# The low part of a weight piece made by one subtraction of 1024 columns, in place of two of 512

## The chip, the cores and the metric

The kernel runs on one core of a Trainium2 chip, as one program. The metric is the time of one execution on the device, in microseconds (us); the span is the part of it that the profiler covers. The engines are TensorE (PE; PEld is its weight load), VectorE (DVE), ScalarE (ACT), GpSimd (POOL) and SyncE (SP), which here only issues transfers. Each engine works through its own instructions in order and waits for others by semaphores.

## What is computed

Two layers of a decoder trunk on 256 tokens with 1024 features, all in float32:

```python
mod = silu(c) @ w_ada + b_ada;  shift, scale, gate = split(mod, 3)
h = rms_norm(x, pre_g) * (1 + scale) + shift
qa, ka, va, ga, qb, kb, vb, gb = split(h @ w_in)      # 8 chunks of 512 columns
# partial rotary on q and k; 8 heads of 64 in each branch
o_a = mixture_of_three_causal_windows(qa, ka, va) * silu(ga)
o_b = causal_block_attention(qb, kb, vb) * silu(gb)   # 256 tokens: one block
y = rms_norm(concat(o_a, o_b) @ w_out, post_g)
x = x + gate * y
```

## The kernel before, in words

**Weights.** All weights lie in HBM as float32 and are read once, 70 MB in all. SP loads them in pieces of 512 KB, `raw` of 128 partitions x 2 k-tiles x 512 columns, into a ring of 6 buffers (line 121 for W_in and W_out, line 142 for W_ada). A piece is only loaded once the piece six before it has been read for the last time, mostly by DVE.

**The split.** TensorE multiplies float32 weights here as two parts. `split_piece` (line 198) has ACT make the high part `whi`, a copy in a shorter format of all 1024 columns (line 205), and calls `split_low` (line 209), which has DVE make the low part, `wlo = raw - whi` (line 212). There are 9 buffers for `whi`, 8 for `wlo`. Each k-tile then takes three matmuls of 512 columns: whi with the high part of h, whi with its low part, wlo with the high part (`product`, line 513; for the gate chunks with weights and h changed over, line 526; in the start line 753). In the start some pieces are split one half at a time, by steps `f` and `g` of a list; later `split_half` takes whole pieces.

**Modulation.** Pieces of W_ada are not multiplied on TensorE. DVE folds each, scaled by silu(c), into an accumulator (line 364, `acc_g` for the gate and `acc_ss` for shift and scale, 1024 columns each), and then ACT and DVE split the gate's sum and TensorE adds it up (lines 444 to 455).

**A head pair.** The stages of a pair of heads hang together over four engines. T: PE transposes q and k into one bank of PSUM (line 571), of which there are two; ACT copies (`qkh` 577, `qkT` 578), DVE makes `qkl` (579), which frees the bank. S: PE makes scores (592, 595). DVE adds the mask and takes the row's minimum (`z`, `den`, 601); ACT takes Exp with sums (604); DVE takes the reciprocal (`rc`, 608) and scales three of four blocks of z (614), ACT the fourth (612). X: PE transposes z in two groups of three (625) into the same two banks, so the second group waits for the `qkl` of the next pair; ACT copies (`pT`, 628). V: PE makes outputs (642), ACT copies them (650). When the gate chunk is there, ACT makes `gs` with Silu (561), DVE multiplies (660), ACT and DVE split (667, 668). Exp and Silu stand in different tables of ACT, so a change between them costs a table load, which the profile shows as ACT_TABLE_LOAD with the line of the instruction behind it.

**Order.** The start, about 60 us, is written out for all engines. After it, only PE's order is that of the program text: products in slots, with stages T, S, X and V of eight head pairs a layer at set slots. The orders of DVE, ACT, POOL and SP are made by the framework's scheduler from its own estimates of when operands are ready, so that a change in one instruction can change the order of others. Layer 0's eight head pairs lie at about 63 to 153 us, the layer boundary at 153 to 190, layer 1 at 190 to 315.

Of the kernel before, what the change touches and what calls it, by code (L numbers as in the profile page):

```python
# [9 lines left out]
F32 = mybir.dt.float32  # L10
# [8 lines left out]
RD = 16  # L19
RH = RD // 2  # L20
EPS = 1e-6
BIG = 1e30
# Slots: one product of half a chunk each, counted in a layer up to 32. Pairs of values: one for each layer.
# Where the heads of a branch start, and the distance of scores, transposes and outputs from there
AT_A, AT_B = ((12, 10), (22, 22))
# where branch A is gated; where the gate and the second token tile's h are made
AO = (28, 27)
AO2 = (0, 2)
GATE_D = (3, 1)
OS, OX, OV = ((1, 1), (3, 3), (4, 5))  # L30
# buffers for weights as loaded and for their two parts
NRAW, NHI, NLO = (6, 9, 8)
FOLD = 2048
# how far the splitting of weights runs ahead; what goes to the scalar engine; where W_ada's parts are due
AHEAD = (-12, 4)
# [3 lines left out]
ADA0, ADA1, ADA2 = ((2, 1), (6, 1), (23, 2))  # L39
# The start. GROUPS: k-tiles whose modulation is made together. FIRST_LOADS: a, b W_ada of a group, f a k-tile of  # L40
# W_in for the first two chunks, s, v quarters of chunks 2 and 5. FIRST_STEPS: T small inputs, R rotary tables, K masks,
# n, x norm and transposes of x, a, b, m modulation of a group, h, l its h in two parts, f, g a weight piece in two
# parts, p its products, w, y and s, v the same for chunks 2 and 5, k products that keep the array busy.
GROUPS = ((0, 1), (1, 1), (2, 2), (4, 2), (6, 2))
# [5 lines left out]
GATE_AT = (21, 27)  # L50
# theta ** (-2 i / RD) in float32
INV_FREQ = [1.0, 0.1939227432012558, 0.03760603070259094, 0.007292664609849453,
# [4 lines left out]
def turn_constants():  # L57
    """For units 2^20, 2^8, 2^-4: frac(unit / 2 pi) cut into parts of 12 bits, over the unit."""
    from fractions import Fraction
    pi = Fraction("3.14159265358979323846264338327950288419716939937510582097494459230781640628620899")  # L60
    rows = []
    for e in (20, 8, -4):
        u = Fraction(2) ** e
        f = u / (2 * pi)
        f -= f.numerator // f.denominator
        f1 = Fraction((f * 4096).numerator // (f * 4096).denominator, 4096)
        g = f - f1
        f2 = Fraction((g * 2 ** 24).numerator // (g * 2 ** 24).denominator, 2 ** 24)
        f3 = g - f2
        rows.append([float(f1 / u), float(f2 / u), float(f3 / u)])  # L70
    return rows
# [3 lines left out]
def trunk(ctx: ExitStack, tc: tile.TileContext, x, c, positions, pre_gain, post_gain,  # L75
# [18 lines left out]

    # ---------------------------------------------------------------- small inputs
    # rows: positions, c, the gains of the first norm, the shift and scale parts of b_ada
    NR = NT + KT + L * KT + 2 * L * KT
# [13 lines left out]

    # ---------------------------------------------------------------- weight stream
    raw_q = {}
# [5 lines left out]
    def load_weights(src, key, r0, c0):  # L119
        """Two k-tiles of 512 columns"""  # L120
        nc.sync.dma_start(piece(key), src[r0:r0 + 2 * P, c0:c0 + CW].rearrange("(k p) n -> p k n", p=P))

    def load_first(key):
        """A k-tile for the first two chunks"""
        k = key[1]
        nc.sync.dma_start(piece(key).rearrange("p c n -> p (c n)"), w_in[0, k * P:(k + 1) * P, 0:2 * CW])

    def load_group(key):
        """W_ada's columns for the shift and scale of a group of features: some of the rows"""
        _, g, q = key  # L130
# [7 lines left out]
    def load_ada(key):  # L138
        """i < KT: a k-tile, the shift or the scale of all features; else the gate, a k-tile"""
        _, l, i, s = key  # L140
# [23 lines left out]

    # Order of the weight stream: with each layer's products, what the next modulation needs.
    # a, b: W_ada for a group of features; f: the rows of W_in that it scales; s, v: quarters of other chunks
    stream = []
    for x in FIRST_LOADS.split():
# [6 lines left out]
        else:  # L175
            stream.append(("in", 0, 2 if i == "s" else 5, g, m))
    # what the modulation needs, after the halves named
    ADA_AT = {}
# [19 lines left out]
    def split_piece(key, a, b, low=True):  # L198
        """Parts a to b of a piece: hi holds the first 12 bits of each weight, lo the other 12."""
        load_upto(key)  # L200
# [8 lines left out]
    def split_low(key, a, b):  # L209
        raw, hi, lo = raw_q[key], hi_q[key], lo_q[key]  # L210
        for d in range(a, b):
            nc.vector.tensor_sub(lo[:, d, :], raw[:, d, :], hi[:, d, :].bitcast(F32))  # L212

# [4 lines left out]

    # ---------------------------------------------------------------- constants
    ident = cp.tile([P, P], F32, name="ident")  # L220
# [5 lines left out]
    dummy = cp.tile([P, 1], F32, name="dummy")  # L226
    # the table set of Silu serves until the first Exp
    nc.scalar.activation(dummy, nhalf, AF.Silu)
    onesr = cp.tile([P, P], F32R, name="onesr")
    nc.scalar.activation(onesr, ones, AF.Copy)  # L230

    # masks, to be added to minus the scores: [queries 0-127 x keys 0-127 | queries 128-255 x keys 0-255]
    NS = P + S
# [29 lines left out]

    # silu(c) and the gains of the first norm by feature on partitions
    cs = cp.tile([P, KT], F32, name="cs")
# [18 lines left out]
    def make_rope():  # L284
        # rotary tables: the angle in turns, reduced exactly, for any position
        invf = cp.tile([P, RH], F32, name="invf")
# [46 lines left out]

    # ---------------------------------------------------------------- modulation
    acc, mod = {}, {}
# [30 lines left out]
    def mod_of(l, part, nb=4):  # L366
        """Rows 0, 32, .. of part in columns: [feature in its block, block, row]."""
        pm = ps.tile([P, CW], F32, name="t", bufs=2)
# [10 lines left out]
    def ada_sum(l):  # L379
        """Sums over partitions of acc; 512 features to each group of 32 columns of the array."""  # L380
        assert all((l, i) in folded for i in range(KT))
# [66 lines left out]
    def gate_end(l, h):  # L448
        """Sums over partitions of acc, on every partition, times the gain of the second norm."""
        pm = ps.tile([P, CW], F32, name="o", bufs=1)  # L450
# [5 lines left out]

    # ---------------------------------------------------------------- norms
    def rstd_of(ms, other=None):
        """(sum of means + EPS) ** -0.5"""
        e = ap.tile([P, 2], F32, name="rstd", bufs=4)  # L460
# [9 lines left out]
    def parts_of(l, g):  # L470
        """hi and lo of half the features of h (or of a branch's output), for all tokens"""
        if (l, g) not in hT:
# [30 lines left out]

    # ---------------------------------------------------------------- products with weights
    def product(bank, act, t, key, first, last, part=None):
        """The four k-tiles of a half, or two of them."""
        if key + (0 if part is None else part,) not in hi_q:
# [8 lines left out]
    def gate_product(bank, act, u, key, hf):  # L516
        """Features 256 u to 256 (u + 1) of a chunk on partitions, all tokens: the weights stay, h streams."""
        if key + (0,) not in hi_q:
# [10 lines left out]

    # ---------------------------------------------------------------- attention  # L530
    qk, vv, gs, qkT, oo = {}, {}, {}, {}, {}
# [35 lines left out]
    def st_T(br, p):  # L567
        pt = ps.tile([P, CW], F32, name="t", bufs=2)
        for i in range(2):
            for t in range(NT):  # L570
                nc.tensor.transpose(pt[:, (2 * i + t) * P:(2 * i + t + 1) * P],
                                    qk[br, i][:, t, p * P:(p + 1) * P], ident)
        # the first 128 queries and keys; for the others, queries and all keys in two parts
        d = ap.tile([P, 2, P], F32, name="qkT", bufs=2)
# [59 lines left out]
    def st_V(br, p):  # L634
        """Outputs of two heads: [feature, token]"""
        res = pT.pop((br, p))
# [18 lines left out]
    def finish(br, p, src=None):  # L655
        """Outputs of two heads times the gate, in two parts"""
        heads.remove((br, p))
# [36 lines left out]

    # ---------------------------------------------------------------- the program
    xT, xn0 = [], []
# [45 lines left out]
    def first_product(q, j, ci):  # L742
        """k-tile 2 q + j with chunk ci, both token tiles"""
        whi, wlo = hi_q["first", 2 * q + j], lo_q["first", 2 * q + j]
# [13 lines left out]
    def early(t, part):  # L758
        """The first half of chunk 5, kept in the memory until the second one is due."""
        if not parked:  # L760
# [32 lines left out]
    def keep_clock(n):  # L793
        """Products that nothing reads: the array's clock stays down until it has been busy for a while."""
        pt = ps.tile([P, CW], F32, name="s", bufs=2)
# [133 lines left out]
```

## Time and profile before

| | us |
|---|---|
| median of 3 runs | 322.24 (322.04 to 323.86) |
| span of the profiled execution | 321.5 |
| PE busy | 299.6 (93%) |
| DVE busy | 245.6 (76%) |
| ACT busy | 203.5 (63%) |
| DVE, the 160 subtractions of line 212 | 102.4 |
| ACT, the 88 copies of line 205 | 84.4 |

A row of a timeline gives start, duration, engine, line, operation, out<-in with sizes; in brackets the idle time before it and who ended it. [...] The granted clock of TensorE was at its higher level (1.00) in all stretches that matter here.

### The profile page before, as it was taken

Reading aid. Unit: us, or ns where it says so; the run is one execution under the profiler, and the core shown is the slowest. Engines: PE = TensorE matmul, PEld = TensorE weight load, DVE = VectorE, ACT = ScalarE, POOL = GpSimd, SP = SyncE. Lnnn points to the kernel's source line nnn. Section 1 sums busy time; section 2 is a strip of 40 time slices with the busy share of each in tenths; the row PEclk is TensorE's granted clock in tenths of the full one; section 3 lists DMA queues with packets and bytes.
Section 4 is the critical chain, followed back from the end, with each engine's and each line's share of the span. In section 5 each row is a group of like instructions: output and inputs, shape, how many; then the busy total and the mean of one; then the engine's idle time right before and its main releaser. Section 6 shows DMA issues by size and latency. Waiting matters only on the chain.

```text
span 321.5 us, 5293 instructions
## 1 busy us (share of the span) xinstructions
PE 299.6 (93%) x1817; PEld 237.6 (74%) x1817; DVE 245.6 (76%) x637; ACT 203.5 (63%) x435; POOL 12.3 (4%) x46
## 2 busy tenths in 40 slices
PE   0898899989999999999999899999999999999992
PEld 0565475867777789877687688877777799997881
DVE  4866773998998989898879899789785566786122
ACT  3646161959777469879568457578675579984100
POOL 3100001000000000000020300000000000000001
PEclk9999999999999999999999999999999999999998
DMA  8999988899798787586858549997765433000011
GB/s 253 342 351 302 346 262 308 293 348 317 247 302 265 259 287 202 173 280 233 285 185 282 178 129 303 350 320 231 228 215 177 132 132 131 2 1 2 0 65 65
DMA packets 37394, 70.63 MB, mean 220 GB/s; under 512 B 2492, under 2 KB 12790, under 8 KB 37368
## 3 DMA queue, kind: packets, MB, share of 16 engines
q1 hardware_dynamic: 36960, 69.22, 65.7%
q10 hardware_dynamic: 408, 1.09, 0.9%
q8 instruction: 14, 0.23, 0.3%
q14 instruction: 12, 0.10, 0.1%
HBM read 69.24 MB, written 1.05 MB: 219 GB/s over the span
## 4 chain that ended last, share of the span: by engine, by line
PE 57%; DMA 14%; DVE 13%; ACT 10%; issue 2%; SPq 1%; POOL 1%; ACTq 0%; DVEq 0%; POOLq 0%
PE mm L513 31%; PE mm L526 7%; DMA raw<-in_w_in_dram 5%; DVE wlo L212 4%; DMA raw<-in_w_ada_dram 4%; ACT whi L205 4%; DMA raw<-in_w_out_dram 3%; PE mm L753 3%; ACT z L604 3%; PE o L642 3%; PE o L414 2%; PE t L625 2%; DVE acc_ss L364 2%; DMA rows<-in_b_ada_dram 1%; PE t L513 1%
## 5 line engine op out<-in xcount | busy, mean ns | idle before, releaser
L212 DVE TENSOR_TENSOR wlo<-raw,whi 128x512 fp32r<-128x512 f32 x160 | 102.4, 685 | 8.0 <-PE mm L513 3.1
L205 ACT ACTIVATE whi<-raw 128x1024 fp32r<-128x1024 f32 (+1 forms) x88 | 84.4, 979 | 37.2 <-DMA raw<-in_w_in_dram 19.8
L513 PE MATMUL mm<-whi,hi 128*128 128x512 f32 x200 | 81.7, 408 | 0.0
L513 PE MATMUL mm<-wlo,hi 128*128 128x512 f32 x200 | 79.1, 395 | 0.0
L513 PE MATMUL mm<-whi,lo 128*128 128x512 f32 x200 | 79.0, 395 | 0.0
L513 PEld LDWEIGHTS mm<-whi,hi 128*128 128x128 f32 x200 | 37.6, 188 | 10.5 <-issue 1.7
L513 PEld LDWEIGHTS mm<-wlo,hi 128*128 128x128 f32 x200 | 37.6, 188 | 8.8
L513 PEld LDWEIGHTS mm<-whi,lo 128*128 128x128 f32 x200 | 37.7, 189 | 8.1 <-DVE lo L502 0.5
L526 PE MATMUL mm<-hi,whi 128*128 128x256 f32 x128 | 37.2, 291 | 0.0
L526 PE MATMUL mm<-hi,wlo 128*128 128x256 f32 x128 | 36.1, 282 | 0.0
L526 PE MATMUL mm<-lo,whi 128*128 128x256 f32 x128 | 36.0, 281 | 0.0
L604 ACT ACTIVATE z<-z,den 128x128 f32<-128x128 f32 x64 | 28.3, 445 | 3.8 <-DVE den L601 3.8
L526 PEld LDWEIGHTS mm<-hi,whi 128*128 128x128 f32 x128 | 24.1, 188 | 1.2 <-issue 0.2
L526 PEld LDWEIGHTS mm<-lo,whi 128*128 128x128 f32 x128 | 24.2, 189 | 0.2
L526 PEld LDWEIGHTS mm<-hi,wlo 128*128 128x128 f32 x128 | 24.1, 188 | 0.0
L364 DVE SCALAR_TENSOR_TENSOR acc_g<-raw,cs,acc_g 128x1024 f32<-128x1024 f32 x16 | 20.5, 1281 | 4.1 <-DMA raw<-in_w_ada_dram 4.1
L687 DVE TENSOR_TENSOR tmp<-mm,gate 128x512 f32<-128x512 f32 x8 | 5.5, 688 | 16.8 <-ACT sq L685 16.8
L364 DVE SCALAR_TENSOR_TENSOR acc_ss<-raw,cs,acc_ss 128x1024 f32<-128x1024 f32 x14 | 17.5, 1276 | 0.0
L685 ACT ACTIVATE sq<-mm 128x512 f32<-128x512 f32 x8 | 4.7, 593 | 19.8 <-PE mm L513 19.8
L625 PE MATMUL t<-ident,z 128*128 128x128 f32 x96 | 15.0, 282 | 2.4 <-DVE qkl L579 1.1
L625 PEld LDWEIGHTS t<-ident,z 128*128 128x128 f32 x96 | 10.6, 140 | 6.2 <-issue 1.7
L628 ACT ACTIVATE pT<-t 128x384 f32<-128x384 f32 x32 | 14.0, 491 | 1.2 <-PE t L625 1.2
(173 smaller groups left out, 454.9 us busy)
## 6 DMA issues: line engine op xcount, KB each, us to landing
raw<-in_w_in_dram SPq DMA_DIRECT2D x64, 512.0 KB, 5.2
raw<-in_w_ada_dram SPq DMA_DIRECT2D x32, 512.0 KB, 4.7
raw<-in_w_ada_dram SPq DMA_DIRECT2D x32, 256.0 KB, 5.0
raw<-in_w_out_dram SPq DMA_DIRECT2D x16, 512.0 KB, 5.1
xs<-in_x_dram SPq DMA_DIRECT2D x2, 512.0 KB, 4.3
gate<-in_post_norm_gain_dram ACTq DMA_DIRECT2D x2, 512.0 KB, 4.9
out_dram<-xs SPq DMA_DIRECT2D x4, 256.0 KB, 2.1
rows<-in_b_ada_dram ACTq DMA_DIRECT2D x2, 8.0 KB, 4.9
```

What stands on the lines that cost most here:

```text
L205: nc.scalar.activation(hi_q[key][:, a:b, :], raw[:, a:b, :], AF.Copy)
L212: nc.vector.tensor_sub(lo[:, d, :], raw[:, d, :], hi[:, d, :].bitcast(F32))
L364: nc.vector.scalar_tensor_tensor(a[:, sl], r[:, sl], cs[:, k:k + 1], a[:, sl], op0=ALU.mult, op1=ALU.add)
L414: nc.tensor.matmul(pm[32 * j:32 * j + 32, :w], csz[:, k, :], r[:, i * w:(i + 1) * w], start=k < 4, stop=k >= 4, tile_position=(0, 32 * j))
L513: nc.tensor.matmul(bank, a[:, k, t, :], w[:, k % 2, :], start=first and k + i == 0, stop=last and k == KH - 1 and i == 2)
L526: nc.tensor.matmul(bank[:, b * S:(b + 1) * S], w[:, k % 2, c0:c0 + P], a[:, k].rearrange("p t q -> p (t q)"), start=hf + b + k + i == 0, s ...
L604: nc.scalar.activation(z[:, a:b], z[:, a:b], AF.Exp, bias=den[:, 0, t, i:i + 1], scale=-1.0, accum_out=den[:, 1, t, i:i + 1])
L625: nc.tensor.transpose(pt[:, b * P:(b + 1) * P], pp[i][:, b * P:(b + 1) * P], ident)
L628: nc.scalar.activation(d, pt[:, :NS], AF.Copy)
L642: nc.tensor.matmul(ob[i * HD:(i + 1) * HD, q0:q0 + P], v[:, t, h], res[i][:, c0:c0 + P], start=t == 0, stop=n != 1, tile_position=(0, i * HD))
L687: nc.vector.tensor_mul(yg[:, sl], yb.pop((t, cc)), gate[l][:, sl])
L753: nc.tensor.matmul(mm[0, ci, t], a[:, k, t, :], w[:, ci, :], start=q == 0 and j == 0 and i == 0, stop=q == 3 and j == 1 and i == 2)
```

## The change

In `split_low` the loop over the k-tiles of a piece is gone: one `tensor_sub` takes all the columns that the call is for. For a whole piece that is 1024 columns in place of two times 512. Calls for one half (steps `g` of the start) stay as they are.

```diff
     def split_low(key, a, b):
         raw, hi, lo = raw_q[key], hi_q[key], lo_q[key]
-        for d in range(a, b):
-            nc.vector.tensor_sub(lo[:, d, :], raw[:, d, :], hi[:, d, :].bitcast(F32))
+        nc.vector.tensor_sub(lo[:, a:b, :], raw[:, a:b, :], hi[:, a:b, :].bitcast(F32))
```

Comments were taken out at the same time; from line 212 on, a line's number is one lower than before. The order of PE's and of SP's instructions is the same in both kernels. Those of DVE and ACT differ.

On ACT at the first head pair of layer 0 the order was this (`vv` is the copy of a value chunk; the rows from the table load on are Exp, then the copies of the next pair's q and k):

```order
L557 ACTIVATE vv<-t 128x512
L205 ACTIVATE whi<-raw 128x1024
L604 ACT_TABLE_LOAD
L604 ACTIVATE z,den<-z,den 128x128
L604 ACTIVATE z,den<-z,den 128x256
L604 ACTIVATE z,den<-z,den 128x128
L604 ACTIVATE z,den<-z,den 128x256
L577 ACTIVATE qkh<-t 128x384
L578 ACTIVATE qkT<-t 128x256
L205 ACTIVATE whi<-raw 128x1024
L612 ACTIVATE z<-z,rc 128x256
```

It is now this, with the second `whi` ahead of the table load, where it stood behind the copies of q and k:

```order
L556 ACTIVATE vv<-t 128x512
L205 ACTIVATE whi<-raw 128x1024 x2
L603 ACT_TABLE_LOAD
L603 ACTIVATE z,den<-z,den 128x128
L603 ACTIVATE z,den<-z,den 128x256
L603 ACTIVATE z,den<-z,den 128x128
L603 ACTIVATE z,den<-z,den 128x256
L576 ACTIVATE qkh<-t 128x384
L577 ACTIVATE qkT<-t 128x256
L205 ACTIVATE whi<-raw 128x1024
L611 ACTIVATE z<-z,rc 128x256
```

On DVE at the same pair, from behind its `den` on, the order was this (the numbers tell buffers apart: raw_889 and raw_891 are pieces of W_ada, raw_994 and raw_1001 the two next weight pieces):

```order
L364 SCALAR_TENSOR_TENSOR acc_g_795<-raw_889,cs_108,acc_g_795 128x1024
L212 TENSOR_TENSOR wlo_997<-raw_994,whi_996 128x512
L364 SCALAR_TENSOR_TENSOR acc_g_795<-raw_891,cs_108,acc_g_795 128x1024
L608 RECIPROCAL rc_770<-den_759 128x4
L212 TENSOR_TENSOR wlo_997<-raw_994,whi_996 128x512
L614 TENSOR_SCALAR z_760<-z_760,rc_770 128x128
L614 TENSOR_SCALAR z_760<-z_760,rc_770 128x256
L614 TENSOR_SCALAR z_765<-z_765,rc_770 128x128
L579 TENSOR_TENSOR qkl_819<-t_812,qkh_818 128x384
L212 TENSOR_TENSOR wlo_1004<-raw_1001,whi_1003 128x512 x2
L364 SCALAR_TENSOR_TENSOR acc_g_795<-raw_1008,cs_108,acc_g_795 128x1024
```

It is now this (raw_881, raw_984, raw_990 and raw_996 are the former raw_891, raw_994, raw_1001 and raw_1008). The split of the second piece has moved ahead of `rc`, and a fold stands between `rc` and the three z:

```order
L363 SCALAR_TENSOR_TENSOR acc_g_787<-raw_881,cs_108,acc_g_787 128x1024
L211 TENSOR_TENSOR wlo_987<-raw_984,whi_986 128x1024
L211 TENSOR_TENSOR wlo_993<-raw_990,whi_992 128x1024
L607 RECIPROCAL rc_764<-den_753 128x4
L363 SCALAR_TENSOR_TENSOR acc_g_787<-raw_996,cs_108,acc_g_787 128x1024
L613 TENSOR_SCALAR z_754<-z_754,rc_764 128x128
L613 TENSOR_SCALAR z_754<-z_754,rc_764 128x256
L613 TENSOR_SCALAR z_759<-z_759,rc_764 128x128
L578 TENSOR_TENSOR qkl_811<-t_804,qkh_810 128x384
```

On ACT at the sixth pair, where the first Silu of layer 0 comes behind that pair's Exps, the order was this (raw_1788 is the first piece of W_out):

```order
L604 ACTIVATE z_1399,den_1393<-z_1399,den_1393 128x256
L561 ACT_TABLE_LOAD
L561 ACTIVATE gs_1458<-mm_1286 128x512
L612 ACTIVATE z_1399<-z_1399,rc_1404 128x256
L650 ACTIVATE oo_1467<-o_1460 128x256
L577 ACTIVATE qkh_1475<-t_1469 128x384
L578 ACTIVATE qkT_1474<-t_1469 128x256
L667 ACTIVATE hi_1609<-oo_922 128x256 x2
L205 ACTIVATE whi_1790<-raw_1788 128x1024
```

It is now this (raw_1764 is the former raw_1788). That piece's `whi` stands ahead of the table load; the same has happened at the eighth pair with a later piece:

```order
L603 ACTIVATE z_1381,den_1375<-z_1381,den_1375 128x256
L205 ACTIVATE whi_1766<-raw_1764 128x1024
L560 ACT_TABLE_LOAD
L560 ACTIVATE gs_1438<-mm_1270 128x512
L611 ACTIVATE z_1381<-z_1381,rc_1386 128x256
L649 ACTIVATE oo_1447<-o_1440 128x256
L576 ACTIVATE qkh_1455<-t_1449 128x384
L577 ACTIVATE qkT_1454<-t_1449 128x256
```

## Rows read from the trace of the kernel before

**Rows 1.** Busy time by stretch: from:to, length, each engine (count), PE's clock, DMA share.
```profile
63.00:153.00 90.00, 86.97 (x612) 71.63 (x611) 83.88 (x220) 67.92 (x158) 0.95 (x1) 1.00 0.82 266
...
190.00:315.00 125.00, 124.63 (x782) 103.40 (x780) 85.68 (x229) 81.46 (x175) 0.86 (x2) 1.00 0.45 148
...
sum 321.50, PE 299.62 PEld 237.64 DVE 245.65 ACT 203.47 POOL 12.30; mean PE 59.92 PEld 47.53 DVE 49.13 ACT 40.69 POOL 2.46
```

**Rows 2.** Waits of PE, 63 to 153 us: total, times, longest.
```profile
PE t L571 <- DVE qk L550: 1.0, 1, 1.0
PE t L625 <- DVE z L614: 0.8, 2, 0.5
PE t L625 <- DVE qkl L579: 0.7, 3, 0.3
PE t L625 <- ACT z L612: 0.4, 1, 0.4
```

**Rows 3.** Waits of PE, 190 to 315 us.
```profile
PE t L625 <- DVE qkl L579: 0.4, 1, 0.4
```

**Rows 4.** Waits of DVE, 63 to 153 us.
```profile
DVE rc L608 <- ACT z L604: 3.7, 4, 1.4
```

**Rows 5.** The page's costliest groups: count, busy, mean ns, idle time before.
```profile
L212 DVE TENSOR_TENSOR wlo<-raw,whi 128x512 fp32r<-128x512 f32 x160 | 102.4, 685 | 8.0 <-PE mm L513 3.1
```

**Rows 6.** The chain of waits, 55 to 163 us, rows for prices: start, us, what.
```profile
90.73 1.20 DVE acc_g L364
...
120.45 2.41 DVE wlo L212 x4
...
134.24 0.34 DVE oo L660
```

**Rows 7.** Busy time by stretch, line 212 alone.
```profile
63.00:153.00 90.00, 26.50 (x41) 1.00 0.82 266
```

**Rows 8.** Timeline of DVE at the end of layer 0.
```profile
158.18 3.10 DVE L212 TENSOR_TENSOR wlo<-raw,whi 128x512 fp32r<-128x512 f32 x5
```

**Rows 9.** Timeline of PE at the end of layer 0.
```profile
161.74 0.40 PE L513 MATMUL mm<-wlo,hi 128*128 128x512 f32 x1
```

**Rows 10.** The chain of waits at head 0.
```profile
72.27 1.06 ACT whi L205
...
73.35 1.28 ACT L604
...
76.55 0.18 DVE rc L608
...
77.22 0.73 DVE z L614 x3
77.96 0.48 DVE qkl L579
```

**Rows 11.** Timeline of SP, the issue of the second piece at head 0.
```profile
68.58 0.38 SPq L121 DMA_DIRECT2D raw<-in_w_in_dram  x1
```

**Rows 12.** Transfers of line 121 from 67 to 76 us.
```profile
DMA to landing us min/median/max: 4.5/4.5/5.1
```

**Rows 13.** The chain of waits at heads 4 to 7.
```profile
115.64 0.95 ACT whi L205
116.59 1.37 ACT z L604 x6
...
125.79 5.31 DMA raw<-in_w_out_dram
...
148.15 0.41 ACT z L612
```

**Rows 14.** Timeline of PE at head 0, the second transposes of z.
```profile
78.48 0.33 PE L625 MATMUL t<-ident,z 128*128 128x128 f32 x1 [0.22 <-DVE qkl L579]
```

**Rows 15.** Timeline of ACT at head 5.
```profile
125.74 1.28 ACT L561 ACT_TABLE_LOAD   x1
```

## The prediction, made blind

> **What bounds the kernel now.** I read the busy time by stretches first [rows 1]. Over the whole span TensorE (PE) is busy 299.6 of 321.5 us, VectorE (DVE) 245.65. The stretches say where that mean comes from: in 63 to 153 us (layer 0 after its hand-ordered start, eight head pairs, called heads 0 to 7 here) PE is busy 86.97 of 90 us and DVE 83.88; in 190 to 315 (layer 1) PE is busy 124.63 of 125 and DVE only 85.68. So layer 1 is PE's alone, and layer 0 is shared: PE is nearly full, and DVE has 6 us to spare in 90.
>
> Next I read what PE waited for. In 63 to 153 its waits add up to 2.9 us: 1.0 for the last rotary result (qk, L550), 0.8 and 0.4 for the scaled probabilities z of a head (DVE L614, ACT L612), 0.7 for qkl (L579) [rows 2]. In all of layer 1 it is 0.4 [rows 3]. PE never waits for wlo, the very thing that the change makes. What a faster subtraction can give is therefore only what it lets DVE do sooner for the heads; and DVE's own largest wait in that stretch is for ACT's Exps, 3.7 us [rows 4], which the change does not speed up.
>
> **The price of the new instruction.** Before, 160 subtractions of 128x512 take 102.4 us, 685 ns of duration each [rows 5]. What one costs DVE is the distance to the next start: four in a row take 2.41 us, so 0.60 each; a tensor-by-tensor operation of 256 columns takes 0.34 [rows 6]. Between the two, 256 columns more cost 0.26; so 1024 columns cost 0.60 + 2 x 0.26 = 1.13, against 1.20 for two of 512. That saves 0.08 a pair. The nearest row of that width is a fold (L364, 1024 columns, two operands and a factor): 1.20 [rows 6], which would save nothing. I take 1.13, since the narrower rows are of the same operation; the bounds are 0 and 0.08. Of the 160, 16 are single halves of the start and stay; 72 pairs are merged: 72 x 0.08 = 5.8 us of DVE in all. In 63 to 153, where DVE is nearly full, lie 41 subtractions [rows 7], some 20 pairs: 1.6 us. In layer 1 it is idle time on an engine that already has 39 us of it: 0.
>
> What a merged subtraction loses is an early first half: the low part of the first k-tile is there 1.13 - 0.60 = 0.53 later than before. That matters where wlo is used soon after it is made. The tightest place is the end of layer 0: five subtractions in a row end at 161.28 [rows 8], the last two of them a pair, and PE uses the first of that pair at 161.74 [rows 9]. Merged, both halves are ready when the second one is now, still 0.46 ahead of the use. So I count 0 there; at worst, with a split that comes later in the new order, 0.5.
>
> [...]
>
> **The order.** The larger part of the change is not in its line. PE's and SP's orders are hand-set or stay the same; DVE's and ACT's are made by the framework's scheduler, and they come out otherwise (the excerpts above). Three places count.
>
> Head 0. On ACT a second whi now stands ahead of the table load for Exp. Before, the load began at 73.35, right behind the first whi (72.27) [rows 10]. The second whi's piece was issued at 68.58 [rows 11] and lands 4.5 to 5.1 later [rows 12]: 73.1 to 73.7. A whi holds ACT for 0.95 (115.64 in [rows 13]), so the load begins at 74.2 to 74.6, 0.8 to 1.3 later, and the reciprocal rc moves from 76.55 to about 77.7. On DVE a fold (1.20) now stands between rc and the three z (L614), where before it was the rest of a 512 subtraction: rc to z took 77.22 - 76.55 = 0.67 and now takes 0.09 + 1.20 = 1.29, which is 0.6 more. Behind z stands qkl of head 1, and PE's second group of transposes (78.48) waits for it, because it needs the bank that qkl frees. PE already waited 0.22 there [rows 14], so the whole delay shows: 1.4 to 1.9; I take **+1.7**.
>
> Heads 1 to 6. In heads 1 to 3 the z stand 1 to 2 us of DVE work later in the order, but PE comes 1.7 later too and had no wait at any of the three: 0. At heads 4 to 6 PE's waits of before for z (0.8) and for qkl (0.7 [rows 2], of which 0.2 at head 0) are covered by PE's own lateness: 0.8 + 0.7 - 0.2 = **-1.3**.
>
> Head 5. On ACT a whi of W_out stands ahead of the table load for Silu, which began at 125.74 [rows 15]; its piece was issued only at 125.79, when a fold of DVE had freed its buffer, and took 5.31 to land [rows 13]. In the new order that fold stands ahead of head 5's scores on DVE, where before it stood behind them. Counted from head 4's rc, before it come a split, z, qkl and a gate product: 1.13 + 0.73 + 0.48 + 0.60 + 1.20 for the fold itself = 4.1. That rc follows the Exps, which ended at 117.97 with a whi of 0.95 in their midst [rows 13] that now stands elsewhere: rc at 117.0 to 118.0, fold done at 121.2 to 122.1, piece landed at 126.5 to 127.4, whi done 0.95 later, and the load 1.7 to 2.6 late. I take 1.8. PE is late itself by then (1.7 less 0.3 for head 4 and 0.3 for head 5, of the above); the rest is new: **+0.7**. With a piece that lands at 131.1, as before, it would be +5.
>
> Head 7. A whi again stands ahead of the Silu load, behind which come gs and the z of ACT at 148.15 [rows 13]. PE waited for that z already, the 0.4 in [rows 2], so a whi of 0.95 shows whole: **+0.9**.
>
> The start: four merged splits, each of which waits for its whi and not for DVE; at most 4 x 0.08: **-0.1**. Layer 1: **0**; a split now stands ahead of z at its first head, where the only wait of PE lies [rows 3], so at worst +0.5.
>
> Sum: 1.7 - 1.3 + 0.7 + 0.9 - 0.1 = +1.9. The profiled execution has a span of 321.5; the median of the runs is 322.2, 0.7 above it. 321.5 + 1.9 + 0.7 = **324.1 us**.
>
> **The rivals.**
> A, DVE's time comes back. The orders matter little, and DVE hands the heads over sooner: PE's waits in layer 0 (2.9) go, and the 0.3 of the start: 322.2 - 3.2 = 319.0; half of it gives 320.6. For it: DVE is busy 83.88 of 90 us in that stretch [rows 1], and 1.5 of the waits are on its z and qkl. Against: these stand behind ACT's Exps, and the first 1.0 is for rotary work right behind the start's merged splits, which wait for their whi. Chance 0.10. [...]
> B, nothing moves. PE's stream covers both the gain and the new order; then 321.2 to 322.8. For it: waits of 3 us in 90 say that the slack is small, but at heads 1 to 3 it is there. Against: at head 0 PE had no slack at all. Also the case where the merged operation costs the fold's 1.20 and the scheduler's moves cancel. Chance 0.20.
> C, as worked out: a loss at heads 0, 5 and 7, half returned at 4 to 6: 322.8 to 325.5. Chance 0.45.
> D, slower. The whi at head 5 waits for its piece in front of the Silu load. It decides once the piece lands after about 127; each us later is a us of PE, since the load, gs, z and qkl of the next head follow one another on ACT. At 129 to 131 it gives 322.2 + 1.7 + 2 to 5 = 326 to 329. For it: ACT's largest waits in this stretch are for pieces, and before, this one came at 131.1. Against: its buffer is freed earlier in the new order. Chance 0.25.
>
> **How the numbers follow.** 324.1 is C's. About 1% (3.2 us) is what a measurement of this kernel tells from no change: 319.0 to 325.5. Below 319.0 lies the better half of A, 0.05; above 325.5 lies D, 0.25; the rest, 0.70, is within. The range 320.5 to 327.0 leaves out most of A (0.07) and half of D (0.12). C's own range is 322.8 to 325.5.
>
> **What would show it.** In the new profile: a merged subtraction with a duration of about 1.22 us and a distance of 1.13 (at 1.20 it saves nothing); at head 0 the Exp table load at 74.2 to 74.6 and PE's second transposes near 80.2; at head 5 the Silu load at 127.5; no waits for z and qkl at head 4; PE's waits in 63 to 153 at about 4 to 5 us in place of 2.9; layer 1 of the same length. It would be wrong if PE reached head 4 no later than before (A or B), or if a whi held the Silu load past 129 (D).

## The result and the profile after

| | before | changed |
|---|---|---|
| median of the runs, side by side | 322.44 us (322.04 to 323.86) | 327.5 us (326.2 to 328.1, 4 runs) |
| profiled execution | 322.24 us | 327.88 us |
| span of it | 321.5 us | 325.9 us |

The ratio is 1.014, with a 95% interval of 1.009 to 1.018: slower by 0.9 to 1.8%. The forecast was 324.1 us, no change that can be measured, with a range of 320.5 to 327.0. The median lies 0.5 us above the range's upper end; the ratio times the median shown of before (322.24) gives 326.7, just inside it. Of the executions behind the numbers below, four lie more than 1.5% above the fastest of their kernel and are left out of the ratios, though not of the medians: one of the first kernel with the operation alone (373.84 us, mean clock 0.76), two of the second order set by hand (327.95 and 327.75 us) and one of the kernel before (325.57 us).

The page of the changed kernel: engines, granted clock by slices of 8.1 us, and the group of the new operation (columns as in [rows 5]).

```profile
PE 300.9 (92%) x1817; PEld 239.5 (73%) x1817; DVE 241.6 (74%) x565; ACT 204.7 (63%) x435; POOL 14.5 (4%) x46
...
PEclk9979999999799999999999999999999999999998
...
L211 DVE TENSOR_TENSOR wlo<-raw,whi 128x1024 fp32r<-128x1024 f32 (+1 forms) x88 | 97.0, 1122 | 9.5 <-PE mm L512 4.2
```

160 subtractions have become 88 (72 pairs and the 16 single halves), and DVE's busy time fell by 4.0 us. The clock row has a 7 in the third slice and a 7 in the eleventh (81 to 90 us).

Busy time by stretch (columns as in [rows 1]):

```profile
63.00:153.00 90.00, 85.34 (x594) 71.19 (x594) 84.28 (x198) 68.11 (x158) 1.50 (x1) 0.98 0.84 283
...
190.00:315.00 125.00, 124.46 (x779) 103.13 (x779) 86.82 (x207) 84.54 (x180) 0.87 (x2) 1.00 0.45 149
```

Against [rows 1] PE has lost 1.6 us of busy time in the 90 us of layer 0 and stands at a clock of 0.98; layer 1 is nearly as full as before. What PE waited for, in 63 to 153, 153 to 190 and 190 to 326 us (columns as in [rows 2]):

```profile
PE t L624 <- DVE z L613: 2.2, 1, 2.2
PE t L624 <- ACT z L611: 1.0, 1, 1.0
PE t L570 <- DVE qk L549: 0.9, 1, 0.9
PE t L624 <- DVE qkl L578: 0.6, 2, 0.4
...
PE t L491 <- ACT tmp L482: 1.7, 1, 1.7
...
PE t L624 <- DVE qkl L578: 0.3, 1, 0.3
PE t L624 <- DVE z L613: 0.2, 1, 0.2
```

In 63 to 153 the waits are 4.7 us, against 2.9 in [rows 2]; 2.2 of them are one wait for z, at head 0. Here is head 0 in the timelines of ACT, DVE and PE (start, us, engine, line; in brackets the idle time before and what ended it):

```profile
74.39 1.06 ACT L205 ACTIVATE whi<-raw 128x1024 fp32r<-128x1024 f32 x1 [0.91 <-DMA raw<-in_w_in_dram]
75.47 1.28 ACT L603 ACT_TABLE_LOAD   x1
...
78.67 0.18 DVE L607 RECIPROCAL rc<-den 128x4 f32<-128x4 f32 x1 [0.98 <-ACT z L603]
78.76 1.27 DVE L363 SCALAR_TENSOR_TENSOR acc_g<-raw,cs,acc_g 128x1024 f32<-128x1024 f32 x1
79.95 0.74 DVE L613 TENSOR_SCALAR z<-z,rc 128x128 f32<-128x128 f32 x3
...
80.37 0.61 PE L624 MATMUL t<-ident,z 128*128 128x128 f32 x3 [2.15 <-DVE z L613]
81.21 0.55 PE L624 MATMUL t<-ident,z 128*128 128x128 f32 x3 [0.22 <-DVE qkl L578]
```

The second whi waits 0.91 us for its piece in front of the table load, a fold stands between rc and z (1.28 us from the one to the other), and PE waits. And this is what followed for PE, by stretches:

```profile
78.10:81.80 3.70, 1.32 (x9) 0.77 (x10) 3.13 (x7) 3.70 (x9) 0.00 (x0) 1.00 0.97 335
81.80:85.30 3.50, 3.50 (x16) 2.79 (x17) 3.50 (x11) 2.09 (x9) 0.00 (x0) 0.51 0.87 282
85.30:88.70 3.40, 3.40 (x26) 2.60 (x25) 2.91 (x9) 1.80 (x6) 0.00 (x0) 1.00 0.94 327
```

PE was busy in 1.32 of 3.70 us; in the 3.5 us behind that it had a granted clock of 0.51 and got through 16 matmuls, where the next 3.4 us, at 1.00, hold 26.

PE's order is the same in both kernels, so the start of each of its 1817 matmuls can be set beside the start of the same one before. How late PE is in the profiled execution, and where that changes (us):

| place | before | changed | late by | step |
|---|---|---|---|---|
| heads' first transposes of q, k | 67.51 | 68.13 | 0.62 | +0.6, in the start |
| head 0, transposes of z | 77.65 | 80.37 | 2.73 | **+2.1** |
| products behind them | 81.01 | 85.25 | 4.24 | **+1.5**, clock at 0.51 |
| head 4, z | 119.71 | 123.31 | 3.60 | -0.6 |
| head 6, z | 139.53 | 141.98 | 2.45 | -1.2 |
| head 7, z | 148.60 | 151.63 | 3.03 | +0.6 |
| layer boundary, transposes of tmp | 184.51 | 188.41 | 3.90 | **+0.9** |
| layer 1, first head, z | 218.20 | 222.63 | 4.43 | +0.5 |

The last line is the difference of the two spans, 4.4 us. The 0.6 of the start is not in an instruction that the change touches first: PE's waits there end with transfers, and one more drop of the clock (0.50 from 17.0 to 20.4 us) falls into the changed kernel's start in this execution; I do not ascribe it to the change. A second profiled execution of the changed kernel (below) bears this out: its span is 324.4 us, 2.9 above that of before, with its heads' first transposes 0.6 earlier than before (66.88) in place of 0.6 later. From there to the end PE loses 3.6 us in it and 3.8 in the first.

### The profile page after: what moved, and what is told of

It reads as the page before. It is cut to its first block, busy times and chain, and to the rows that moved or that the text cites. A ratio compares the mean times of both kernels' runs of the same rounds, so it can differ in the third digit from the quotient of the medians.

```text
span 325.9 us, 5225 instructions
## 1 busy us (share of the span) xinstructions
PE 300.9 (92%) x1817; PEld 239.5 (73%) x1817; DVE 241.6 (74%) x565; ACT 204.7 (63%) x435; POOL 14.5 (4%) x46
## 4 chain that ended last, share of the span: by engine, by line
PE 64%; ACT 11%; DMA 10%; DVE 7%; issue 3%; POOL 2%; SPq 1%; ACTq 0%; DVEq 0%; POOLq 0%
PE mm L512 36%; PE mm L525 7%; DMA raw<-in_w_ada_dram 4%; PE mm L752 3%; PE o L641 3%; ACT whi L205 3%; DMA raw<-in_w_in_dram 3%; PE t L624 3%; PE o L413 2%; ACT z L603 2%; DMA raw<-in_w_out_dram 2%; PE t L570 2%; PE s L591 1%; DVE acc_ss L363 1%; DMA rows<-in_b_ada_dram 1%
## 5 line engine op out<-in xcount | busy, mean ns | idle before, releaser
L211 DVE TENSOR_TENSOR wlo<-raw,whi 128x1024 fp32r<-128x1024 f32 (+1 forms) x88 | 97.0, 1122 | 9.5 <-PE mm L512 4.2
```

The lines of the kernel that those rows point to most:

```text
L211: nc.vector.tensor_sub(lo[:, a:b, :], raw[:, a:b, :], hi[:, a:b, :].bitcast(F32))
```

## The experiments

**The method.** Except for the second run of the changed kernel, these kernels fix the order of DVE and ACT. Behind the program text a list of numbers gives for each of the two engines the order in which its instructions are issued, and each one is tied to the one ahead of it by an order edge without a semaphore; PE's order stays that of the program text. So the operation and the order can be changed one at a time. The edit is shown by its place in that order, in rows of the change's excerpts.

```diff
+        force_order(tc, {mybir.EngineType.DVE: DVE_ORDER, mybir.EngineType.Activation: ACT_ORDER})
```

Theory: the order makes the loss, mostly at head 0, and the operation itself costs nothing. Rival: the merged operation itself costs, because both halves of wlo come late or DVE is held longer at a stretch.

### The order alone

The split stays at two subtractions of 512, in the places where the changed kernel has one of 1024.

```diff
 def split_low(key, a, b):      # as before
     for d in range(a, b):
         nc.vector.tensor_sub(lo[:, d, :], raw[:, d, :], hi[:, d, :].bitcast(F32))
+DVE_ORDER, ACT_ORDER: those of the changed kernel, each 1024 split replaced by its two halves
```

> The two subtractions of 512 columns stay, but DVE and ACT issue everything in the order of the changed kernel (each merged subtraction's place is taken by its two halves). If the order alone makes the loss (theory 1), PE stands still for about 2 us at the first head pair, 0.9 more than before at the layer boundary, gains some 1.5 us back at heads 4 to 6, and the time is 324 to 328 us, near the changed kernel's 327.5. If the wide instruction itself makes it (theory 2), the time is within 1 us of the kernel before (322.4), with no stall at the first head pair.

328.15 us against 323.1, ratio 1.017 (1.012 to 1.021). PE's waits, and the stretch behind head 0:

```profile
PE t L625 <- DVE z L614: 2.1, 1, 2.1
...
PE t L492 <- ACT tmp L483: 2.1, 2, 1.9
...
81.80:85.30 3.50, 3.50 (x17) 2.79 (x18) 3.50 (x12) 2.03 (x8) 0.00 (x0) 0.59 0.92 309
```

The whole loss is there without the new operation: the wait at head 0, the lower clock behind it, and the longer wait at the boundary (1.9 us for tmp, against 1.0 before). The rival falls.

### The operation alone, in two places

The order of before is kept, with each pair of halves replaced by one subtraction. Where something stood between the halves, it has to be chosen on which side the whole goes. First: where the second half stood (`op_alone`); then: where the first half stood (`op_first`). At the end of layer 0:

```diff
 second half's place:
-L211 wlo_1845 first half of the k-tiles
 L667 lo_1710<-oo_1447,hi_1709
+L211 wlo_1845, 1024 columns
 first half's place:
+L211 wlo_1845, 1024 columns
 L667 lo_1710<-oo_1447,hi_1709
-L211 wlo_1845 second half of the k-tiles
```

> The subtraction of 1024 columns, with DVE and ACT in the order of the kernel before (the wide one stands where the second half stood). Theory 1 (order): 320.5 to 322.5 us, no stall of 1 us at the first head pair, the granted clock as before; DVE's busy time about 4 us less. Theory 2 (the wide instruction): 324 us or more.

> The subtraction of 1024 columns in the order of the kernel before on DVE and ACT, as in op_alone, but it now stands where the first of the two halves stood. In op_alone PE waited 1.6 us for wlo at the end of layer 0. If that was a matter of the place (there the whole pair stood behind a wait for ACT that only its second half had stood behind), that wait goes and the time is 320.5 to 323.5 us, that of the kernel before (323.1 on this chip). If the wide instruction is late by its width, PE still waits for wlo there for 0.5 us or more and the time stays near op_alone's 325.8.

The first gave 325.76 us, ratio 1.007 (1.003 to 1.011), and not the gain that was expected. Its timelines of PE and DVE at the end of layer 0:

```profile
161.17 0.51 PE L512 MATMUL mm<-wlo,hi 128*128 128x512 f32 x1 [1.64 <-DVE wlo L211]
...
159.56 0.43 DVE L667 TENSOR_TENSOR lo<-oo,hi 128x256 fp32r<-128x256 f32 x1 [2.29 <-ACT hi L666]
159.90 3.49 DVE L211 TENSOR_TENSOR wlo<-raw,whi 128x1024 fp32r<-128x1024 f32 x3
```

One half had stood ahead of a subtraction (lo) that waits 2.29 us for ACT. Moved behind it, the split came late and PE waited 1.64 us for wlo: in the lists of PE's waits of all these kernels the only one for what the change makes.

The second gave 321.19 us against 322.75, ratio **0.995 (0.992 to 0.997)**. PE's waits in 63 to 155 and 155 to 193:

```profile
PE t L624 <- DVE z L613: 0.9, 1, 0.9
PE t L570 <- DVE qk L549: 0.8, 1, 0.8
PE t L624 <- DVE qkl L578: 0.7, 3, 0.2
PE t L624 <- ACT z L611: 0.2, 1, 0.2
...
PE t L491 <- ACT tmp L482: 0.7, 1, 0.7
```

So the operation by itself gains 1.6 us. In the profiled execution (span 320.3 us against 321.5) PE gains 0.6 us at head 4 and 0.6 at head 7, where its waits of before for z are gone, and 0.5 at the boundary; it loses 0.2 at head 0 and 0.4 at head 6. That DVE reaches its z sooner there fits this, but was not tested by itself.

The two parts add up about: 1.017 for the order and 0.995 for the operation give 1.011; the change measured 1.014. In the profiled spans the order has +5.5 us (327.0) and the operation -1.2, together 4.3, and the change 4.4. A kernel in which an order is fixed and nothing else changes was not run. If fixing cost or gave time by itself, it would be in both parts and twice in their sum, so the sum speaks against it as far as the parts add up.

### What head 0 costs, and which part of the order makes it

Three kernels put back parts of head 0 in the changed kernel's order: the second whi with its split, the fold, or both with what follows from them.

```diff
 ACT, whi put back:
-L205 whi x2            +L205 whi
 L603 ACT_TABLE_LOAD, Exps, L576 qkh, L577 qkT
-L205 whi               +L205 whi x2
 DVE, fold put back:
 L607 rc
-L363 acc_g
 L613 z x3, L578 qkl
+L363 acc_g
```

> The changed kernel with the second whi of the first head pair alone put back behind the copies of the next pair (and its split on DVE behind qkl, since it needs that whi); the fold stays between rc and z. By the prediction's terms whi costs 0.8 to 1.3 of the stall and the fold 0.6: PE's waits at this pair fall from 2.6 us (2.2 for z, 0.4 for qkl) to 1.0 to 1.6. If the fold is the larger part, they stay above 1.8.

> The changed kernel with the fold between rc and z of the first head pair alone moved behind qkl; the whi stays ahead of the table load. By the prediction's terms 0.6 us of the stall go: PE's waits at this pair fall from 2.6 us to about 2.0. If they fall to 1.2 or less, the fold was the larger part (it takes 1.2 on DVE).

> The changed kernel with its first head pair alone put back: on ACT the second whi behind the copies of the next pair's q and k, on DVE the split of that piece and a fold behind qkl of the next pair, as before. If the stall there brings both its own 1.9 us and the fall of PE's granted clock right behind it (1.5 us), PE's wait of 2.2 us for z goes, the clock stays at its higher level there, and the time falls by 2 to 3.5 us to 324 to 325.5; what the changed kernel got back at heads 4 and 6 shrinks, since PE arrives earlier. If the clock falls for another reason, only 1 to 2 us come back.

The first two ran once each: 324.36 us with the whi put back, 324.84 with the fold put back, beside 323.19 of before. Head 0 in them and in the third: with the whi put back, ACT's whi ahead of its z, and PE; then PE with the fold put back; then PE with both:

```profile
78.15 1.06 ACT L205 ACTIVATE whi<-raw 128x1024 fp32r<-128x1024 f32 x1 [0.67 <-DMA raw<-in_w_in_dram]
...
79.66 0.44 PE L624 MATMUL t<-ident,z 128*128 128x128 f32 x2 [0.87 <-ACT z L611]
...
78.71 0.61 PE L624 MATMUL t<-ident,z 128*128 128x128 f32 x3 [1.43 <-ACT qkT L577]
...
78.72 0.44 PE L624 MATMUL t<-ident,z 128*128 128x128 f32 x2 [1.16 <-ACT z L611]
```

PE's waits at head 0 add up to 1.1 us with the whi put back and to 1.9 with the fold put back, against 2.4 in the changed kernel. These are 1.3 and 0.5 less, near the prediction's terms (0.8 to 1.3, and 0.6). They are no clean prices, though, since the waits that are left are others. With the whi put back, the wait for DVE's z is gone although the fold still stands ahead of it: the Exp table load begins 0.62 us earlier than in the kernel before (72.73 against 73.35), because the first piece landed earlier in this execution, and that covers the fold. What PE waits for is ACT's z: two whi now stand ahead of it, where the kernel before has one, and the second waits 0.67 us for its piece. With the fold put back, PE waits for ACT's qkT, which stands behind the late Exps. In neither execution did the clock go below 1.00 in 63 to 153.

With both put back the runs spread over two groups: 324.4 to 324.9 in three, the profiled one among them, and 325.9 to 328.4 in seven, at mean clocks of 0.994 to 0.996 in the one and 0.984 to 0.992 in the other; ratio 1.011 (1.007 to 1.015). The 324 to 325.5 us that were expected came in three executions of ten. The profiled one has no wait for DVE's z and no stretch at the lower clock in layer 0's heads (1.00 over 63 to 153), and is 1.3 us above the median of before. But it waits 1.16 us for ACT's z, again behind two whi, so this is not head 0 as it was before. Where the clock fell in the other seven cannot be read, since they were not profiled. Putting head 0 back thus took the stall away, but what that gives in time is not shown: 1.011 lies inside the interval of the changed kernel.

### Is it the stall itself, or the clock behind it?

The changed order stays; nine matmuls that nothing reads keep PE busy ahead of head 0's transposes of z.

```diff
+    if not filled:
+        pf = ps.tile([P, CW], F32, name="o", bufs=1)
+        for _ in range(9):
+            nc.tensor.matmul(pf..., onesr, onesr[:, None, :].to_broadcast([P, 4, P]), start=True, stop=True)
     for ...: nc.tensor.transpose(...)      # line 624
```

> The changed kernel, in its own order on DVE and ACT, with 9 matmuls that nothing reads put on PE in front of the first head pair's transposes of z, about 2 us of work in the place of the wait. The stall's length for the program stays. If it is PE's idleness there that brings the clock down, the clock stays at its higher level behind it and the time falls by about 1.5 us in the runs that had the fall; if the fall has another cause, it stays, and the time is that of the changed kernel (327.5) or up to 0.5 more.

325.48 us against 323.1, ratio 1.009 (1.005 to 1.012). The two stretches that showed the stall and the lower clock:

```profile
78.10:81.80 3.70, 3.09 (x22) 2.01 (x21) 3.70 (x7) 3.25 (x6) 0.00 (x0) 1.00 0.99 350
81.80:85.30 3.50, 3.50 (x25) 2.53 (x23) 3.50 (x12) 2.54 (x10) 0.00 (x0) 1.00 0.90 276
```

PE is busy in 3.09 of the 3.70 us, the clock stays at 1.00, and in the next 3.5 us 25 matmuls pass where it were 16. The ratio falls from 1.014 to 1.009, some 1.6 us. In the order of DVE and ACT nothing differs from the changed kernel, so the lower clock follows from PE's idleness; its 1.5 us in the table above are a third of the loss. The intervals of the two ratios overlap; it is the two stretches that show this, and not the time.

The changed kernel itself, a second time, without a list of orders:

> The changed kernel once more, beside the others on this chip: 327 to 328 us if the loss belongs to the program, with a mean granted clock of 0.986 to 0.996 by the number of times that PE's clock fell in an execution.

326.76 us, ratio 1.014 (1.010 to 1.018). The stall (2.0 us for z) and the stretch behind it come again:

```profile
80.80:84.20 3.40, 3.40 (x13) 2.59 (x12) 3.40 (x11) 1.99 (x9) 0.00 (x0) 0.51 0.95 305
```

### The layer boundary: GpSimd

The 0.9 us at 184.51 was in no step of the prediction. There, GpSimd makes rstd (lines 463 and 464), the norm's factor, between the norm's sums and tmp, which PE waits for. The timelines of GpSimd and DVE in the changed kernel:

```profile
181.04 1.22 DVE L211 TENSOR_TENSOR wlo<-raw,whi 128x1024 fp32r<-128x1024 f32 x1
...
184.44 2.35 DVE L211 TENSOR_TENSOR wlo<-raw,whi 128x1024 fp32r<-128x1024 f32 x2
...
181.28 1.15 POOL L463 TENSOR_SCALAR rstd<-ms 128x1 f32<-128x1 f32 x1 [7.97 <-ACT sq L684]
...
185.99 0.97 POOL L463 TENSOR_SCALAR rstd<-ms 128x1 f32<-128x1 f32 x1 [2.92 <-ACT tmp L480]
```

and at the same two places before, with PE's wait:

```profile
178.13 0.68 DVE L687 TENSOR_TENSOR tmp<-mm,gate 128x512 f32<-128x512 f32 x1
...
180.40 2.49 DVE L212 TENSOR_TENSOR wlo<-raw,whi 128x512 fp32r<-128x512 f32 x4
...
178.09 0.30 POOL L464 TENSOR_SCALAR rstd<-ms 128x1 f32<-128x1 f32 x1 [8.72 <-ACT sq L685]
...
181.95 1.11 POOL L464 TENSOR_SCALAR rstd<-ms 128x1 f32<-128x1 f32 x1 [2.92 <-ACT tmp L481]
...
PE t L492 <- ACT tmp L483: 1.0, 1, 1.0
```

An operation on one column takes 0.30 us beside DVE's multiply by the gate, and 0.97 to 1.15 in the other cases, and in each of these it ends 0.17 us or less after DVE's run of splits. The new order has put a split beside the first of the two, which had none: +0.85 us, and PE's wait for tmp is 1.7 us where it was 1.0. In the next kernel the changed order stays, but no split stands beside either.

```diff
-L211 wlo
 L686 tmp<-mm,gate
 L690 xs x2
-L211 wlo x2
+L211 wlo
 L483 tmp<-xs,rstd
+L211 wlo x2
```

> The changed kernel with one thing moved: at the layer boundary no split stands on DVE while GpSimd makes the second token tile's two rstd (three splits moved behind them). In the changed kernel's trace these two operations of one column took 1.15 and 0.97 us, and each ended 0.17 us behind the end of the splits that DVE was at, where one took 0.30 while DVE did not split. If a split keeps GpSimd out until it is done, both take about 0.30, PE's wait for tmp (L482) falls from 1.7 us to 0.5 or less, and PE is 1.2 to 1.5 us earlier from there on. If their length has another cause, they stay at about 1 us and PE's wait at 1.7.

```profile
181.77 0.30 POOL L463 TENSOR_SCALAR rstd<-ms 128x1 f32<-128x1 f32 x1 [7.97 <-ACT sq L684]
...
185.63 0.30 POOL L463 TENSOR_SCALAR rstd<-ms 128x1 f32<-128x1 f32 x1 [2.92 <-ACT tmp L480]
...
PE t L491 <- ACT tmp L482: 0.2, 1, 0.2
```

The mechanism is shown: both take 0.30 us, and PE's wait went from 1.7 to 0.2. The time did not show it (327.16 us, ratio 1.012, 1.007 to 1.017). In the profiled execution PE gains 0.6 us from head 7 to the transposes of tmp, where the changed kernel loses 0.9. But up to z of layer 1's first head it loses 1.8, where the changed kernel loses 0.5, with a wait for z of 0.8 us in place of 0.2; whether the moved splits cause that was not tested. And this kernel still has head 0's stall, behind which the lower clock lasted twice as long here. So what GpSimd's delay costs the whole program is not shown. The wait for z in layer 1 and the stretch behind head 0:

```profile
PE t L624 <- DVE z L613: 0.8, 1, 0.8
...
79.90:86.80 6.90, 6.68 (x25) 5.15 (x25) 6.77 (x17) 3.33 (x11) 0.00 (x0) 0.51 0.92 299
```

### Orders set by hand

With the order free to choose, I moved folds behind qkl and each z right behind its rc in layer 0, once with two subtractions of 512 and once with one of 1024.

```diff
 head 0, DVE:
-L212 wlo, L364 acc_g, L608 rc, L212 wlo, L614 z x3, L579 qkl
+L212 wlo, L608 rc, L614 z x3, L579 qkl, L364 acc_g
 a later head, DVE:
-L608 rc, L364 acc_ss, L614 z x3
+L608 rc, L614 z x3, L364 acc_ss
```

> The kernel before with two subtractions of 512, DVE and ACT in an order written by hand from its trace: at the rotary front, at heads 0, 3, 4, 5 and 8 the Exps and what follows them stand ahead of splits and folds, and no split stands beside GpSimd's rstd at the boundary. If order is what these kernels differ by, PE's waits of 63 to 190 us (3.9) shrink to 2 or less and the time is 1 to 3 us below the kernel before: 320 to 322 us. If DVE is full there, the waits only move to wlo at the end of layer 0 and the time is the same.

> The same order written by hand, with the subtraction of 1024 columns in the place of the first half. This is the change alone in an order that suits both. If the wide instruction only saves DVE 0.07 us a pair, it is equal to tuned_split or up to 1 us faster, since DVE is nearly full in layer 0; if its late first half costs PE time, it is slower by 0.5 us or more, with PE waiting for wlo.

The first missed its 320 to 322: 324.66 us, ratio 1.006 (1.003 to 1.009). The second, 325.3 us, 1.006 (1.002 to 1.010), cannot be told from the first, and PE has no wait for wlo in it; but it too is slower than the kernel before. In the first, PE's waits in 63 to 155 were these:

```profile
PE o L642 <- ACT pT L628: 2.1, 2, 1.4
PE t L625 <- DVE z L614: 1.4, 1, 1.4
PE t L625 <- DVE qkl L579: 1.2, 3, 0.5
```

PE was 1.8 us earlier than in the kernel before at head 0's z, 0.9 at head 1's and 0.2 at head 2's: what the first head gained, the next two gave back. At head 5 it was 1.4 us earlier again, and at head 6's z 1.5 later: the loss lies between these, with 1.4 us of waiting for pT, which none of the lists above shows, and 1.4 for z. The second had, in its profiled execution (327.95 us, the slowest of twelve), a wait for z of 2.0 us at head 6 and, behind it, a stretch at the lower clock (0.50 over 6.8 us); its median is not explained by that. Which of the moves did the harm was not taken apart.

The last kernel takes the order of before with the merged split in the first half's place, moves one split from beside GpSimd's rstd, and at the first head of layer 1 puts one split behind qkl and ACT's copy qkT ahead of its z.

```diff
 boundary, DVE:
-L211 wlo x2, L483 tmp<-xs,rstd, L211 wlo
+L211 wlo, L483 tmp<-xs,rstd, L211 wlo x2
 layer 1, first head, DVE:
-L211 wlo, L578 qkl, L211 wlo
+L578 qkl, L211 wlo x2
```

> op_first (the subtraction of 1024 columns in the order of the kernel before, in the place of the first half) with two more moves that the runs so far pointed to: at the layer boundary the split beside GpSimd's second rstd moves behind what waits for it, and at the first head of layer 1 a split moves behind qkl. By PE's waits in op_first (0.7 for tmp, 0.5 for qkl) these give 0.5 to 1.2 us: 320.0 to 320.7 us where op_first had 321.2. If PE only stands still elsewhere for them, the time is op_first's.

320.78 us against 323.19, ratio **0.993 (0.990 to 0.996)**: faster than the kernel before and than the changed one. From the operation alone (0.995) it cannot be told, since the intervals overlap, so what the two moves give is not shown. PE waits 0.8 us for qk, 0.4 for qkl and 0.2 for ACT's z in 63 to 155 and 0.4 for tmp in 155 to 193; no wait is listed in layer 1.

## Why the prediction was right in part and wrong in part

The kind of change was named rightly: the order decides, not the line. The sign was the likeliest case's, a loss; the size was wrong, mostly by two terms that stood in the sum at nothing: the clock behind head 0's stall and the layer boundary. Against a span of 321.5 the sum was +1.9 and the profiled execution had +4.4. That the ratio puts the time inside the range at all is luck: the range reached 327.0 for half of rival D, whose mechanism did not occur.

- **The price: right.** 1.13 us from start to start was predicted. Three in a row, starting 1.13 apart, take this in the timeline of DVE:

```profile
169.08 3.49 DVE L211 TENSOR_TENSOR wlo<-raw,whi 128x1024 fp32r<-128x1024 f32 x3
```

  (3.49 - 1.22) / 2 = 1.13, with 1.22 the duration of one, as was said. The 0.60 that the price was built on is a distance between starts as well: the five of [rows 8] take 3.10, and (3.10 - 0.685) / 4 = 0.60.
- **Head 0: right in its parts, 0.4 short.** The table load was said to begin 0.8 to 1.3 later: it began 2.1 later (73.35 in [rows 10], 75.47 now), of which 0.6 is to be taken off, since the second piece was issued that much later (69.21, against 68.58 in [rows 11]); 1.5 is left. rc to z was said to take 1.29 and took 1.28. PE's step was 2.1 for 1.7. The two experiments took 1.3 and 0.5 off PE's waits, but are no clean prices, as said there.
- **What the sum left out at head 0: the clock, +1.5.** The prediction priced the wait and stopped there. A wait of 2.15 us in a stretch that was thin anyway (busy in 1.32 of 3.70 us) brought PE to its lower clock (0.51) for 3.5 us. The kernel before shows no such stretch in its heads (1.00 in [rows 1]), so the trace gave no price; but the step "the whole delay shows" should have asked what PE does right behind it. The filled kernel shows the cause.
- **Heads 4 to 6: right in kind.** -1.8 for -1.3; PE's own lateness covered the waits for z and qkl at heads 4 and 6, as said. The wait for qkl at head 5 stayed (0.36 us), and what exceeds the forecast lies in gaps beside the listed waits.
- **Head 5: wrong, 0 for +0.7.** The whi did not wait for its piece, by a hair: the piece landed at 128.19, later than the 126.5 to 127.4 said, and the whi began right behind the Exps at 128.30. The Silu load followed at 129.36, later than the 127.5 said and past the 129 that the prediction named as a sign of being wrong. But PE was itself 3.6 late by then and not 1.1, so nothing of it reached PE. Rival D's mechanism, a whi that waits for its piece in front of the load, did not occur, though its time did.
- **Head 7: right.** +0.6 for +0.9.
- **The boundary: wrong, +0.9 for 0.** I counted layer boundary and layer 1 as one zero because PE hardly waits in layer 1 [rows 3]; the 37 us between were not looked at, though GpSimd works there on PE's path. The change's order moved a split beside it.
- **Layer 1: +0.5,** the "at worst" of the prediction, at its first head, where, as said there, a split now stands ahead of z.
- **The operation's own gain: under-rated.** The sum gave it -0.1, since "PE never waits for wlo". Rival A said that DVE's time comes back through z and qkl, 1.6 to 3.2 us, at 0.10. With the order kept the time does come back: 1.6 us. Rival A was right on the operation's size, and the new order spent it and more; that it comes back through z and qkl is only partly seen. The prediction should have held operation and order as two terms, each with its own sign.
- **The rival for slower** was tied to one place (head 5). Slower came, at 1.014, but by head 0's clock and the boundary, which no rival had.

Summed over the steps: start +0.7 against the forecast, head 0 +0.4, clock +1.5, heads 4 to 6 -0.5, head 5 -0.7, head 7 -0.3, boundary +0.9, layer 1 +0.5. That is +2.5, which with the forecast's +1.9 makes the 4.4. Another 1.3 us lies in the time outside the span: 0.7 in the first execution of before, 2.0 in that of the changed kernel, but also 2.0 in the later executions of before, so it is no matter of the change.

## What to carry to other kernels

Where a scheduler makes the order, price a change of one line as two: the operation in the old order, and the new order with the old operation. Both can be run, and here they had opposite signs (0.995 and 1.017). The merged operation did best where its first part had stood, above all where something that waits stood between the parts. When a new stall of some microseconds lands on TensorE, price the clock behind it too (here 2.0 to 2.2 us of waiting, and then 3.4 to 6.9 us at 0.50 to 0.59); and look for small GpSimd operations on the path that such subtractions of DVE may stand beside (in the changed kernel 0.30 us without one, 0.97 to 1.82 beside them).

## What the runs showed of the hardware that I had not expected

- **TensorE's clock in mid-kernel.** A wait of 2.0 to 2.2 us for z, in the first of them in a stretch with 1.32 of 3.70 us busy, was followed by 3.4 to 3.5 us at 0.51 of the clock, at the same head in both executions of the changed kernel that were profiled; in the kernel that moved splits at the boundary it was 6.9 us. With the same stretch filled to 3.09 us of 3.70, the clock stayed at 1.00. With waits of 1.1 and 1.9 us in several pieces at that head it stayed there too, in one execution each.
- **GpSimd is held by DVE's subtractions.** A one-column operation of GpSimd that takes 0.30 us where no split runs beside it took 0.97 and 1.15 us beside splits; ten us earlier, beside three splits in a row, it took 1.82, and ended 0.09 us after the last of them:

```profile
170.84 1.82 POOL L463 TENSOR_SCALAR rstd<-ms 128x1 f32<-128x1 f32 x1 [3.12 <-ACT tmp L480]
```

  So it did not get in between one split and the next. DVE's multiply by the gate did not hold it: 0.30 us. What in a split holds GpSimd was not tested.
